# Branch A's projection in seven half-block products, its block sums added up in DRAM

## The chip, the cores and the metric

The kernel runs on one NeuronCore of a Trainium2 chip. The metric is the device time of one execution in microseconds (us). A core has a matrix engine (TensorE, PE in the profile; its weight loads are listed as PEld), a vector engine (VectorE, DVE), a scalar engine (ScalarE, ACT), a general engine (GpSimd, POOL) and an engine that issues transfers (SyncE, SP). Transfers issued by SP and by POOL are carried by 16 DMA engines. Each engine runs its own queue of instructions in order and waits on semaphores for the others.

## The reference

One layer of a streaming encoder is computed for 1024 prompt tokens and 32 sample tokens (1056 in all), model width 1024. The part around the change:

```
ya = attention(...)                      # branch A, 1024 wide (16 heads of 64)
yb = recurrence(...)                     # branch B, 1024 wide (8 heads of 128)
mix = sigmoid(ga) * (ya @ w_br_a) + sigmoid(gb) * (yb @ w_br_b)
x = x + rms_norm(mix @ w_out, g_post_mix)
```

After it come the feed-forward part (`w_up`, a short convolution, `w_down`) and a gated input. Everything is float32. `w_br_a` is 1024 x 1024.

## The kernel before

**Precision.** Every float32 operand is split into a high part (`hi`, rounded to the type that PE takes) and the rest (`lo`). A product takes three passes: hi x hi, hi x lo, lo x hi. `split` and the weight preparation do one copy on ACT and one subtraction on DVE for each operand.

**Layout.** Features lie on the 128 partitions, tokens along the free dimension. A 1024 wide operand is 8 row blocks (k), and the output is made in 8 column blocks (c) of 128 features. For the part after the branches the tokens are cut into four groups of 264 (`G4`, `H = 264`).

**Order.** The stages run one after the other, and PE is fed without a break between them:

1. Input norm, query/key/value products, attention head pair by head pair (i = 0 to 7), with gate products beside it. At the end of each i the result `ya` (128 x 1056) goes to DRAM (`ya_d`, L563).
2. Branch B: `w_in` for the recurrence in a scheme with fewer block products (`unit_pieces`), 8 heads, in small steps ("pieces"). Each head writes `yb_d` (L1384). Beside these pieces, POOL builds block sums of `w_down` in DRAM (`w_sums`, L1435 to 1443): 24 transfers from the weight itself and 8 from sums already built, the later ones adding to what lies there (`accum_op`). `behind(E, V, G)` queues an issue behind the last PE, DVE and POOL instruction written before it.
3. The last gate products (`tail`, three gate blocks before L1478 and three in `stream(tail[3:], small)`, L1485).
4. Branch A's projection (L1507 to 1522), the stage that is changed. `load_split` brings `ya_d` in 32 pieces of 128 x 264 and splits them into `Ra` and `Rb`. For each column block c and token group g a `block` of 8 row blocks times 3 passes = 24 matmuls goes to one of six PSUM banks. The weights are loaded 128 columns at a time (`next_w`, two blocks ahead). DVE then multiplies the bank with the gate (`ta_d`, loaded by SP) and POOL stores the result to `mx_d`. Beside it, `yb_d` is loaded and split into `Ya` and `Yb`.
5. Branch B's projection (L1544 to 1556): the same with `Ya`, `Yb`; the gated product is added to what `mx_d` holds and split into `Ra`, `Rb` again, the operands of `w_out`.
6. `w_out`, norms, the up projection (`up_unit`, 22 units) and the down projection (`d_unit`), both in seven products of half blocks, then the last gate and the output.

**The seven-product form.** A product of 2 x 2 blocks is made with seven block products in place of eight, at the price of sums of blocks on both sides ahead of it and of sums of results behind it. `OPS` puts products 0, 1, 2 in a first phase and 3 to 6 in a second. In the down projection the weight sums come from `w_d` and the operand sums from `s_d`; `d_unit` (L2263) runs one phase for one column block, with products 0 and 2, or 3 and 5, accumulating in the same PSUM double bank.

**Pages.** After attention the SBUF is cut into pages of 8 x 264 floats a partition, eight on the right (`rp`, r0 to r7, where branch B's tiles lay) and eight on the left (`lq`, l0 to l7, where the split input lay). A tile on a page waits until the tiles that had its memory before are released. A tile with `bufs=n` rotates through n buffers in the same way.

Of the kernel before, what the change touches and what calls it, by code (L numbers as in the profile page):

```python
# [59 lines left out]
def layer_kernel(  # L60
# [54 lines left out]
    ya_d = [dp.tile([P, T], F32, name=f"ya_d{i}") for i in range(8)]  # L115
    yb_d = [dp.tile([P, T], F32, name=f"yb_d{i}") for i in range(8)]
    ta_d = [dp.tile([P, T], F32, name=f"ta_d{i}") for i in range(8)]
    tb_d = [dp.tile([P, T], F32, name=f"tb_d{i}") for i in range(8)]
    mx_d = [dp.tile([P, T], F32, name=f"mx_d{i}") for i in range(8)]
# [41 lines left out]
    plan += [rows_cols(w_br_a, 0, c * P, P, KT) for c in range(8)]  # L161
# [151 lines left out]
    with right("ap") as ap:  # L313
# [226 lines left out]
        def values(i, js):  # L540
# [21 lines left out]
            if js[-1] == 8:  # L562
                dma(ya_d[i][:], ya[:])  # L563
# [513 lines left out]
    with right("bp") as bp:  # L1077
# [297 lines left out]
        def group_out(h, g):  # L1375
# [8 lines left out]
            dma(yb_d[h][:, o:o + n], sg[:, :n])  # L1384
# [44 lines left out]
        def more():  # L1429
            limit[0] = n_mix  # L1430
            load_next()
# [5 lines left out]
        for n, (o, a, h, other) in enumerate(w_sums):  # L1437
            for c in range(4):
# [4 lines left out]
                at(8 + 5 * (4 * n + c), w_sum)  # L1443
        for m, (run, ev) in enumerate(pieces):
# [12 lines left out]

    def page(pool, n, shape, name):

        return pool.tile(shape, F32R, tag=f"pg{n}", name=nm(name))  # L1460

    def columns8(pool, n, name):

        t = page(pool, n, [P, 8, H], name)
        return [t[:, k, :] for k in range(8)]
# [3 lines left out]
    def mt(tag, bufs):  # L1469
        return mp.tile([P, H], F32, tag=tag, name=nm(tag), bufs=bufs)  # L1470

    def load_split(src, hi, lo, g, k):
        o, n = G4[g]
        t = mt("ld", 8)
        dma(t[:], src[k][:, o:o + n])
        split(hi[g][k], lo[g][k], t[:])

    with right("mp") as mp:  # L1478
        Ra = [columns8(rp, 2 * g, "Ra") for g in range(4)]
        Rb = [columns8(rp, 2 * g + 1, "Rb") for g in range(4)]  # L1480
        small = {}
        for n in range(32):
            small.setdefault(n * 2 // 11, []).append(
                lambda n=n: load_split(ya_d, Ra, Rb, n // 8, n % 8))
        stream(tail[3:], small)  # L1485
        lctx.close()
        pctx.close()
# [5 lines left out]
        pq = qctx.enter_context(  # L1493
            tc.tile_pool(name="pq", bufs=1, space=PSUM, reuse_waits="tile"))

        def mm_bank():
            return bank(pq, "mm", 6)
# [4 lines left out]
        def block(w, wsl, xh, xl, ks, n):  # L1502
            b = mm_bank()
            product(b[:, :n], w, wsl, xh, xl, ks)
            return b
# [38 lines left out]
        for c in range(8):  # L1544
            if c % 2:
                p_cols(c // 2)
# [1118 lines left out]
```

## Time and profile before

| | us |
|---|---|
| runs shown | 1964.16, 1960.82, 1966.80 |
| median | 1964.16 |
| profiled execution | 1962.71 |
| its span, first to last instruction | 1960.9 |
| mean granted clock of PE | 0.998 |

The profile is of one execution. Its span is 1.8 us shorter than the execution's time; the rest is start and end. A row of the timeline gives the start in us from the span's start, the duration, the engine, the line of the kernel, the operation, the tiles (out<-in) and the shapes, and in brackets how long the engine sat idle before and what ended that. A row of the groups gives the count, then the time in which at least one of them was busy and the mean duration of one in ns, then the idle time of the engine just before them. Matmuls overlap on PE, so the duration of one is longer than the distance from one start to the next. Attention stores its eight results between 119 and 347 us of the span, branch B its results between 444 and 839; branch A's projection runs from 850 to 943, branch B's from there to about 1037.

### The profile page before, as it was taken

The numbers are of one execution on the slowest core, as the hardware profiler recorded it, in microseconds if no ns is written. First come the engines' busy times: TensorE is split into PE (matmuls) and PEld (weight loads), VectorE is DVE, ScalarE is ACT, GpSimd is POOL, SyncE is SP. The second block draws the span as 40 slices with busy tenths as digits, with TensorE's granted clock in tenths as the row PEclk, the third lists the DMA queues.
The fourth block names the chain that finished last, engine by engine and source line by source line (L and its number), as shares of the span: only waits on it lengthen the run. The fifth ranks groups of instructions, "written<-read, shape, count | busy, mean of one in ns | idle before, by whom it ended". The sixth has DMA issues, their size and how long they took to land. (4 is left out here: it accounts for less than half of the span.)

```text
span 1960.9 us, 38386 instructions
## 1 busy us (share of the span) xinstructions
PE 1938.8 (99%) x14715; PEld 1921.4 (98%) x14715; DVE 1432.0 (73%) x3174; ACT 997.9 (51%) x2182; POOL 299.7 (15%) x423
## 2 busy tenths in 40 slices
PE   8999999999999999999999999999999999999998
PEld 7999999999999999999999999999999999999998
DVE  6777777888888888654455778778778786668872
ACT  7667767666656666542224664333333346534432
POOL 2111111011102000002001023343333410000000
PEclk9999999999999999999999999999999999999999
DMA  8533433434549531477558582333323347655443
GB/s 269 148 102 99 128 109 118 156 106 117 115 106 168 110 87 36 136 229 236 167 166 296 174 296 62 111 101 109 110 94 118 96 159 248 206 183 160 120 132 89
DMA packets 296125, 283.12 MB, mean 144 GB/s; under 512 B 14885, under 2 KB 266184, under 8 KB 295941
## 3 DMA queue, kind: packets, MB, share of 16 engines
q1 hardware_dynamic: 270117, 224.80, 37.0%
q0 software_dynamic: 25696, 55.80, 11.7%
q8 instruction: 116, 1.90, 0.4%
q14 instruction: 68, 0.56, 0.1%
q10 hardware_dynamic: 128, 0.06, 0.0%
HBM read 195.46 MB, written 100.28 MB: 151 GB/s over the span
## 5 line engine op out<-in xcount | busy, mean ns | idle before, releaser
L2099 PE MATMUL st<-op,wt 128*128 128x264 f32 x1232 | 349.7, 284 | 3.8 <-ACT Sp L2110 1.7
L2101 PE MATMUL st<-op,wt 128*128 128x264 f32 x1232 | 350.4, 285 | 0.0
L2100 PE MATMUL st<-op,wt 128*128 128x264 f32 x1232 | 348.4, 283 | 0.0
L2099 PEld LDWEIGHTS st<-op,wt 128*128 128x128 f32 x1232 | 231.9, 188 | 5.6 <-ACT Sp L2110 2.3
L2100 PEld LDWEIGHTS st<-op,wt 128*128 128x128 f32 x1232 | 232.1, 188 | 0.0
L2101 PEld LDWEIGHTS st<-op,wt 128*128 128x128 f32 x1232 | 231.6, 188 | 0.0
L2218 PE MATMUL st<-dop,wt 128*128 128x264 f32 x616 | 174.4, 283 | 1.7 <-ACT S L2233 1.7
L2220 PE MATMUL st<-dop,wt 128*128 128x264 f32 x616 | 174.3, 283 | 0.0
L2219 PE MATMUL st<-dop,wt 128*128 128x264 f32 x616 | 173.9, 282 | 0.0
L1763 ACT CAST wt<-wu 128x512 fp32r<-128x512 f32 x126 | 75.9, 619 | 178.1 <-POOL ab L2085 75.5
L201 PE MATMUL mm<-La,wh 128*128 128x384 f32 (+1 forms) x480 | 158.2, 330 | 0.0
L202 PE MATMUL mm<-Lb,wh 128*128 128x384 f32 (+1 forms) x480 | 155.3, 324 | 0.6 <-DVE Lb L771 0.6
L203 PE MATMUL mm<-La,wl 128*128 128x384 f32 (+1 forms) x480 | 154.9, 323 | 0.1
L201 PE MATMUL mm<-Ra,wh 128*128 128x264 f32 x512 | 145.4, 284 | 0.0
L202 PE MATMUL mm<-Rb,wh 128*128 128x264 f32 x512 | 145.0, 283 | 0.0
L203 PE MATMUL mm<-Ra,wl 128*128 128x264 f32 x512 | 145.0, 283 | 0.0
L1764 DVE TENSOR_TENSOR wt<-wu,wt 128x512 fp32r<-128x512 f32 x126 | 86.4, 694 | 46.7 <-ACT wt L1763 46.7
L2218 PEld LDWEIGHTS st<-dop,wt 128*128 128x128 f32 x616 | 115.6, 188 | 2.2 <-ACT S L2233 1.9
L2219 PEld LDWEIGHTS st<-dop,wt 128*128 128x128 f32 x616 | 115.7, 188 | 0.0
L2220 PEld LDWEIGHTS st<-dop,wt 128*128 128x128 f32 x616 | 115.4, 187 | 0.0
L202 PEld LDWEIGHTS mm<-Rb,wh 128*128 128x128 f32 x512 | 96.5, 188 | 0.0
L201 PEld LDWEIGHTS mm<-Ra,wh 128*128 128x128 f32 x512 | 96.4, 188 | 0.0
(577 smaller groups left out, 6005.8 us busy)
## 6 DMA issues: line engine op xcount, KB each, us to landing
wu<-in_w_up_dram SPq DMA_DIRECT2D x42, 512.0 KB
wu<-in_w_in_dram SPq DMA_DIRECT2D x36, 512.0 KB
w_d<-in_w_down_dram POOLq DMA_DIRECT2D x24, 704.0 KB, 10.5
a_d<-Up SPq DMA_DIRECT2D x22, 528.0 KB
wr<-in_w_in_dram SPq DMA_DIRECT2D x21, 512.0 KB
s_d<-sm SPq DMA_DIRECT2D x40, 264.0 KB
dop<-s_d SPq DMA_DIRECT2D x16, 528.0 KB
wr<-in_w_out_dram SPq DMA_DIRECT2D x16, 512.0 KB
```

Of the source, the lines that this page charges most:

```text
L201: E.matmul(ps, wh, a, start=first and n == 0, stop=False)
L202: E.matmul(ps, wh, b, start=False, stop=False)
L203: E.matmul(ps, wl, a, start=False, stop=last and n == len(ks) - 1)
L1763: S.copy(t[:, 0], src)
L1764: V.tensor_tensor(t[:, 1], src, t[:, 0].bitcast(F32), op=ALU.subtract)
L2099: E.matmul(o, wh, xh, start=first and k == 0, stop=False, skip_group_check=True)
L2100: E.matmul(o, wh, xl, start=False, stop=False, skip_group_check=True)
L2101: E.matmul(o, wl, xh, start=False, stop=k == 3, skip_group_check=True)
L2218: E.matmul(o, wh, xh_, start=first and k == 0, stop=False, skip_group_check=True)
L2219: E.matmul(o, wh, xl_, start=False, stop=False, skip_group_check=True)
L2220: E.matmul(o, wl, xh_, start=False, stop=k == ng - 1, skip_group_check=True)
```

## The change

The product `ya @ w_br_a` is cut into 2 x 2 blocks: the 8 row blocks k into two halves (a), the 8 column blocks into two halves (h), and the tokens of each pair of groups t into two halves of 264 (h). It is then made in seven products of half blocks, each of 4 row blocks, for 4 column blocks c and 2 token pairs p. In `a_unit` one weight of 4 row blocks x 128 columns meets one operand of 4 row blocks x 264 tokens in 12 matmuls.

- **Operand sums.** At the end of each head pair in attention, ACT makes negated copies of two 264-token pieces in the two gate buffers (`gtile`), and SP stores them in `sa_d` (24 stores). During branch B, POOL adds the other blocks with five transfers from DRAM to DRAM (`y_sums`), four of them adding.
- **Weight sums.** Eight such transfers build the four sums of `w_br_a` blocks in `wa_d` (`a_sums`), four adding. The 13 transfers stand at every twelfth piece from piece 10 on.
- **Operands.** `a_load` brings 14 operand halves (7 products, 2 token pairs) straight onto pages, eight of them in the last three gate blocks, the other six in the first steps of the stage; `a_split` splits them in place.
- **Weights.** `a_raw` loads two half weights at a time, `a_prepare` splits them up to five ahead. `more` now stops at the gate weights (`n_gates`), and branch B's projection weights are asked for in steps 30 and 32 of 34.
- **Order.** The first two column blocks of phase 0 run for token pair 0 and then for pair 1 (12 half steps), then column blocks 2 and 3, then phase 1. Three PSUM double banks (`st`) replace the six single ones.
- **Results.** DVE combines the products, multiplies by the gate and either stores to `mx_d` (half of the output, through POOL) or keeps the gated result in SBUF (`M_`).
- **Branch B's projection.** Its operands are loaded straight onto pages in steps 18 to 21 and 31 to 32 and split in place, the last ones within branch B's first blocks; the first two column blocks run group by group. It reads `mx_d` for half of the blocks and `M_` for the other half.

The diff, cut to its core:

```diff
@@ attention, values() @@
             if js[-1] == 8:
-                dma(ya_d[i][:], ya[:])
+                dma(ya_d[:, i], ya[:])
+                for p in range(2):
+                    nt, o = gtile(), H * (2 * p + 1 - i // 4)
+                    S.mul(nt[:, :H], ya[:, o:o + H], -1.0)
+                    for q in ((4, 3) if i < 4 else (5,)):
+                        dma(sa_d[q][:, i % 4, p], nt[:, :H])
@@ branch B, beside its pieces @@
+        a_sums = [(3, av[:, 0, 0], 0), (4, av[:, 0, 1], 0), (1, av[:, 0, 0], 0), (6, av[:, 1, 0], 0),
+                  (3, av[:, 0, 1], 1), (4, av[:, 1, 1], 1), (1, wa_d[4][:], 1), (6, wa_d[1][:], 1)]
+        y_sums = [(4, ya_v[:, 0, 0], 1), (3, ya_v[:, 1, 1], 1), (1, sa_d[4][:], 0),
+                  (1, ya_v[:, 1, 1], 1), (5, sa_d[1][:], 1)]
+        for n, (dst, (o, src, acc)) in enumerate([(sa_d, y) for y in y_sums] + [(wa_d, a) for a in a_sums]):
+            def a_sum(dst=dst[o], src=src, op={"accum_op": ALU.add} if acc else {}):
+                with behind(E, V, G):
+                    gdma(dst[:], src, max_dma_last_dim=4224, **op)
+            at(10 + 12 * n, a_sum)
@@ the last gate blocks @@
+    at_a = {0: ("r6", "r5"), 1: ("r1", "r7"), 2: ("r3", "r4"), 3: ("r0", "r2"), 4: ("l0", "l1"),
+            5: ("l2", "l3"), 6: ("l4", "l5")}
+    def a_raw():
+        k = len(raw_a)
+        t = wp.tile([P, KT, P], F32, tag="wr", name=nm("wa"), bufs=2)
+        raw_a.append(t)
+        for a in range(2):
+            c, i = A_ORDER[2 * k + a]
+            src = wa_d[i] if i in wa_d else av[:, i // 2 % 2 + i // 5, i // 5]
+            dma(t[:, 4 * a:4 * a + 4], src[:, :, c * P:(c + 1) * P])
...
+    def a_load(i, p):
+        t = opa[i, p] = page_at(at_a[i][p], [P, 2, 4, H], "oa")
+        src = sa_d[i][:, :, p] if i in sa_d else ya_v[:, min(i, 1), i // 6][:, :, p]
+        dma(t[:, 1].bitcast(F32), src)
+    small = {0: [lambda i=i, p=p: a_load(i, p) for p in range(2) for i in range(3)]}
+    small[0] += [lambda p=p: a_load(3, p) for p in range(2)]
+    for m in range(4):
+        p, i = divmod(m, 3)
+        small.setdefault(m + 2, []).append(lambda i=i, p=p: both(a_split, i, p))
+    for m in range(3):
+        small.setdefault(m + 1, []).insert(0, lambda m=m: both(a_prepare, m))
+    stream(tail[3:], small)
@@ the stage @@
+        def a_unit(ph, c, tps=(0, 1), ws=None, beside=None):
+            X, Y = (pa.tile([P, 2, 512], F32, tag="st", name=nm("st"), bufs=3) for _ in range(2))
+            banks = {0: (X, True), 1: (Y, True), 2: (X, False), 3: (X, True), 4: (Y, True),
+                     5: (X, False), 6: (Y, False)}
...
+            for n, i in enumerate(OPS[ph]):
...
+                    a_prepare(n_a[0] + 5)
...
+                for p in tps:
+                    o, x = t[:, p, 0:H], opa[i, p]
+                    for k in range(4):
+                        E.matmul(o, w[:, 0, k], x[:, 0, k], start=first and k == 0, stop=False,
+                                 skip_group_check=True)
...
+                if i == 0:
+                    d["s"], d["ta"] = tmp("as"), a_gate(c, 0, sl)
+                    S.copy(d["s"][:, sl], x)
+                elif i == 1:
+                    V.tensor_tensor(r, x, d["s"][:, sl], op=ALU.subtract)
+                elif i == 2:
+                    ta = d["ta"]
+                    V.scalar_tensor_tensor(ta[:, sl], ta[:, sl], 1.0, x, op0=ALU.add, op1=ALU.mult)
+                    gdma(mx_d[:, 0, c, sl], ta[:, sl])
...
+        for n, (i, p) in enumerate((i, p) for i in (4, 5, 6) for p in range(2)):
+            during(2 * n, a_load, i, p)
+            during(9 + n + n // 2, both, a_split, i, p)
+        for n, (i, p) in enumerate(((1, 1), (2, 1), (3, 0), (3, 1))):
+            during(n + n // 2, both, a_split, i, p)
+        for n in range(4):
+            during(18 + n, y_load, n // 2, n % 2)
+            during(23 + n, both, y_split, n // 2, n % 2)
+        for n in range(4):
+            during(31 + n // 2, y_load, 2 + n // 2, n % 2)
+        during(30, prefetch)
+        during(32, both, load_next)
...
+        ws = [a_unit(0, c, (0,), beside=beside) for c in range(2)]
+        for c in range(2):
+            a_unit(0, c, (1,), ws[c], beside)
+        for c in range(2, 4):
+            a_unit(0, c, beside=beside)
+        for c in range(4):
+            a_unit(1, c, beside=beside)
```

216 lines of the change are left out of this document (147 added, 69 removed).

## Prediction

> **What bounds the kernel now.** The page's busy times come first, then the granted clock.
>
> ```profile
> PE 1938.8 (99%) x14715; PEld 1921.4 (98%) x14715; DVE 1432.0 (73%) x3174; ACT 997.9 (51%) x2182; POOL 299.7 (15%) x423
> PEclk9999999999999999999999999999999999999999
> ```
>
> TensorE (PE) is busy for 99% of the span at a full clock. Busy time alone does not prove that it is dense, because matmuls overlap in the pipeline, so the second view is the timeline of PE at both ends of the branch A projection (start, duration, engine, line, operation), and the third the groups inside it.
>
> ```profile
> 850.00 0.28 PE L201 MATMUL mm<-Ra,wh 128*128 128x264 f32 x1
> ...
> 942.81 0.28 PE L201 MATMUL mm<-Ya,wh 128*128 128x264 f32 x1
> ```
> ```profile
> L201 PE MATMUL mm<-Ra,wh 128*128 128x264 f32 x256 | 72.6, 284 | 0.0
> L202 PE MATMUL mm<-Rb,wh 128*128 128x264 f32 x256 | 72.5, 283 | 0.0
> L203 PE MATMUL mm<-Ra,wl 128*128 128x264 f32 x256 | 72.5, 283 | 0.0
> ```
>
> The first row is the first matmul of branch A, the second the first one of branch B's projection. Between them lie 3 x 256 = 768 matmuls, so the stage lasts 92.81 us and one matmul costs 92.81 / 768 = 0.1208 us of the span. The 283 ns of the groups is the latency of one, not its cost; whoever takes it would promise 27 us. The last column (idle before) is 0.0: there is no wait in this stage. Every matmul taken out shortens the span, and every wait put in lengthens it.
>
> The fourth view gives stretches (from:to, length, then busy time with count for PE, PEld, DVE, ACT, POOL, then clock, DMA share, GB/s): attention, branch B, the last three gate blocks, and the projection in pieces.
>
> ```profile
> 119.00:385.00 266.00, 264.85 (x1845) 262.46 (x1844) 202.41 (x607) 191.81 (x500) 41.02 (x116) 1.00 0.43 125
> 385.00:838.00 453.00, 452.03 (x3025) 449.50 (x3024) 373.99 (x1042) 284.53 (x749) 48.05 (x73) 1.00 0.47 108
> 838.00:850.00 12.00, 12.00 (x77) 11.96 (x77) 5.21 (x12) 6.28 (x16) 0.00 (x0) 1.00 0.66 196
> 850.00:867.00 17.00, 17.00 (x142) 17.00 (x142) 12.86 (x32) 10.51 (x26) 1.65 (x4) 1.00 0.92 277
> 867.00:885.00 18.00, 18.00 (x151) 18.00 (x150) 7.98 (x18) 6.59 (x14) 3.22 (x6) 1.00 0.81 244
> 885.00:905.00 20.00, 20.00 (x168) 20.00 (x167) 12.18 (x26) 8.50 (x19) 3.76 (x7) 1.00 0.86 262
> ```
>
> Behind PE the next resource in this stage is the DMA engines: 0.92 busy in its first 17 us. That is where the change can give its gain back.
>
> **The change, part by part.** *Removed.* Seven products of 4 column blocks, 2 token pairs, 4 row blocks and 3 passes are 7 x 4 x 2 x 4 x 3 = 672 matmuls of the same shape. 96 go: 96 x 0.1208 = **11.6 us**. The loops fix this count, so I see no way for the change not to do what it says.
>
> [...]
>
> *Added at the opening.* The same seven-product scheme runs twice already. Its first waits, in the down projection and in the up projection (the brackets hold PE's idle time and what ended it):
>
> ```profile
> 1628.15 0.28 PE L2220 MATMUL st<-dop,wt 128*128 128x264 f32 x1
> 1630.11 0.39 PE L2218 MATMUL st<-dop,wt 128*128 128x264 f32 x1 [1.68 <-ACT S L2233]
> ```
> ```profile
> 1163.99 0.39 PE L2099 MATMUL st<-op,wt 128*128 128x264 f32 x1 [0.69 <-ACT ple L1739]
> 1166.44 0.39 PE L2099 MATMUL st<-op,wt 128*128 128x264 f32 x1 [0.73 <-ACT ple L1739]
> 1168.17 0.39 PE L2099 MATMUL st<-op,wt 128*128 128x264 f32 x1 [1.23 <-ACT Sp L2110]
> ```
> ```profile
> L2218 PE MATMUL st<-dop,wt 128*128 128x264 f32 x592 | 167.6, 283 | 1.7 <-ACT S L2233 1.7
> ```
>
> The down projection loses 1630.11 - 1628.15 - 0.12 = 1.8 us at its start and, in the rest of 3 x 592 matmuls, nothing (the 1.7 is that one wait). The up projection waits 2.7 us in three places, on ScalarE's (ACT's) copies out of PSUM. Why the scheme waits where eight plain products do not: product 2 accumulates onto product 0's bank and must wait for its copy, and three double banks replace six single ones. For the new opening I take 2.5 us, bounds 0 (the stage now opens without a wait) and 18 (below).
>
> *VectorE and ScalarE beside it.* The prices of one weight half, one operand half and one evacuation:
>
> ```profile
> L1870 ACT CAST wt<-wd 128x512 fp32r<-128x512 f32 (+1 forms) x84 | 49.0, 586 | 91.0 <-PE st L2220 80.0 <-DMA wd<-w_d 4.8 <-issue 2.6
> L1871 DVE TENSOR_TENSOR wt<-wd,wt 128x512 fp32r<-128x512 f32 (+1 forms) x84 | 53.0, 641 | 6.3 <-ACT wt L1870 6.3
> L2072 ACT CAST dop<-dop 128x1056 fp32r<-128x1056 f32 (+1 forms) x42 | 42.0, 1000 | 2.8 <-DMA dop<-a_d 2.6 <-DMA dop<-s_d 0.2
> L2073 DVE TENSOR_TENSOR dop<-dop 128x1056 fp32r<-128x1056 f32 (+1 forms) x42 | 48.7, 1162 | 14.4 <-ACT dop L2072 14.3
> L1519 DVE SCALAR_TENSOR_TENSOR ta<-ta,mm 128x264 f32<-128x264 f32 x32 | 13.5, 426 | 28.1 <-PE mm L203 16.2 <-DMA ta<-ta_d 11.8
> ```
>
> The first 12 steps are half steps of 12 matmuls, 12 x 12 x 0.1208 = 17.4 us. In them VectorE (DVE) has 8 weight halves, 6 operand halves and 8 evacuations: 8 x 0.641 + 6 x 1.162 + 8 x 0.426 = 15.5 us, or 89%, where it has 12.9 of 17 now. It fits, barely; after step 12 the steps are twice as long. At nothing, therefore, but inside the 2.5.
>
> *DMA of the stage.* Sizes and counts of today's issues:
>
> ```profile
> w_d<-in_w_down_dram POOLq DMA_DIRECT2D x24, 704.0 KB, 10.5
> w_d<-w_d POOLq DMA_DIRECT2D x8, 704.0 KB, 6.7
> wd<-w_d SPq DMA_DIRECT2D x32, 256.0 KB
> ld<-ya_d SPq DMA_DIRECT2D x32, 132.0 KB
> dop<-s_d SPq DMA_DIRECT2D x16, 528.0 KB
> ```
>
> Operands grow from 32 x 132 KB (4.3 MB) to 14 x 528 KB (7.6 MB), weights from 8 x 512 KB (4.2 MB) to 28 x 256 KB (7.3 MB); the gates stay at 4.3 MB, and branch A's stored part halves from 4.3 to 2.2 MB, written once and read once. With branch B's operands (4.3 MB) and next weights (1.3 MB) some 27 MB go through in 81 us (672 x 0.1208) and the 12 us ahead, near 290 GB/s, against the 244 to 277 of the rows. So a part has to come earlier, or the queue runs late. A load can start when the memory of its page is free. Branch B's tiles set that: its block-sum operands (`TH`, `TL`) are last read at 816.6, its output tiles (`sg`) only after 838.7 (first and last start of each group).
>
> ```profile
> L1111 PE MATMUL Y<-TL,wt x216: 333/334/346, 358.7 to 816.6; 128*128 128x384 f32 x108
> L1382 DVE SCALAR_TENSOR_TENSOR sg<-tr,ghh,sg x24: 499/602/771, 443.3 to 838.7; 128x384 f32<-128x384 f32 x16, 128x288 f32<-128x288 f32 x8
> ```
>
> The eight pages (67.6 KB a partition) cover the eight tiles `TH` and `TL` (49.2 KB) and 18.4 KB of the tiles beside them, so about five of them are free some 20 us before the other three. On SP's queue today the loads come behind branch B's last store:
>
> ```profile
> 839.29 0.38 SPq L1384 DMA_DIRECT2D yb_d<-sg  x1
> 839.77 2.31 SPq L1475 DMA_DIRECT2D ld<-ya_d  x5
> ...
> 845.98 0.42 SPq L1517 DMA_DIRECT2D ta<-ta_d  x1
> ```
>
> The last row shows a gate load that overtook `ld` loads waiting for buffers, so the order on SP follows readiness, and I take it that five operand halves are loaded early. The three left at 839.8 (1.6 MB, 6 us at 277 GB/s) land ahead of their products from 850.
>
> *Block sums.* 13 transfers of about 1.06 MB on POOL's queue in branch B; by bytes from the rows above each takes 6.7 to 10.5 x 1.06 / 0.72 = 10 to 15 us, in all 130 to 200 of 453 us. The branch already carries 32 smaller ones and PE is busy 452.03 of 453; DMA share would go from 0.47 to at most 0.9. POOL issues 13 more:
>
> ```profile
> L1442 POOL DMA_DIRECT2D w_d<-in_w_down_dram x24 | 32.2, 1518 | 1.1 <-issue 0.8
> ```
>
> 13 x 1.5 = 20 us more of POOL beside its 48 of 453; memsets and copies queue behind, and PE's banks cover them. I charge 0.5 us, bounds 0 and 8 (third rival). If the cover is gone, a late weight half stops PE.
>
> *Attention.* 16 negated copies on ACT and 24 small stores on SP. A scaled copy of this shape:
>
> ```profile
> L1651 ACT ACTIVATE z<-x,gvec 128x264 f32<-128x264 f32 x28 | 12.3, 508 | 2.1 <-DVE x L1641 2.1
> ```
>
> 16 x 0.508 = 8 us, ACT being busy 191.81 of 266, so they fit. Each also borrows one of the two gate buffers until its stores land; the gate copy and the exponentials queue behind it on ACT. 0.3 us, bounds 0 and 4.
>
> *Hand-over to branch B.* The first two of its weights are prepared in the last four steps (11.6 us), two copies and two subtractions beside PE: 0.4 us, bounds 0 and 3.
>
> **Sum.** -11.6 + 2.5 + 0.5 + 0.3 + 0.4 = -7.9. The profiled execution took 1962.7 (span 1960.9 and 1.8 around), giving 1954.8; the median of the runs, 1964.2, would give 1956.3. I say **1955.5**.
>
> **The rivals.** *First, the gate loads become the wait.*
>
> ```profile
> DVE ta L1519 <- DMA ta<-ta_d: 11.8, 8, 3.6
> ```
>
> Today DVE waits 8 times, 11.8 us in all, for a gate tile. Six banks of one product each (24 x 0.1208 = 2.9 us) hide it. The new evacuation of product 2 needs the same loads, its bank is wanted again one half step (1.45 us) later, and behind it on DVE stand the weight subtractions and every other evacuation. Against it: gate loads overtake others already. If half of these waits reach PE: 5.9 more, 1961.
>
> *Second, the opening is bound by DMA and the kernel gets slower.* Place: steps 0 to 12. If no page is free early, the queue holds from 839.8 the 8 + 6 operand halves (7.6 MB), 10 weight halves (2.6), gates, stores and gate writes (1.7): 11.9 MB at the mean of 277 and 244, 260 GB/s, take 46 us, until 885.6; step 12 is due at 867.4. 18 us late replace the 2.5: 1955.5 + 15.7 = 1971. It decides at 10.4 us late (the 2.5 charged and the 7.9 left), that is, by whether some operand halves are issued before 839: five of them are 2.7 MB, 10 us. For it speaks the 0.92 of the first 17 us; against it the reordering on SP. [...]
>
> *Third, the sums hold up branch B's weights.* Where transfers bunch, one of 10 to 15 us stands before weights asked for about half a unit (12 us) ahead: two such places at 4 us give 8, 1963. PE's 452.03 beside 32 such transfers speaks against it. [...]
>
> **How the numbers follow.** About 0.3%, 5.9 us, is what a measurement of this kernel can tell from no change; faster means below 1958.3. Forecast 0.60 (its own range 1950.5, all waits hidden, to 1958), first rival 0.18, third 0.08, second 0.14. Faster 0.60, same 0.26, slower 0.14. The range goes from 1950 to 1967: below it little is possible with 11.6 removed, above it lies most of the second rival.
>
> **What would show it.** Right: 672 matmuls at 0.121 us between branch A's first and branch B's first, a stage of 82 to 87 us, operand loads on SP before 839, a first wait of 1 to 4 us ended by ACT or DVE. Wrong: gaps in steps 0 to 12 ended by a DMA (second rival) or by DVE behind a gate load (first), or PE's busy time falling in attention or branch B.

## The result and the profile after

The changed kernel takes **1977.4 us** (median of four runs, 1976.8 to 1980.5) where the kernel before takes 1963.8 on the same chip (four runs, 1960.8 to 1966.8): a ratio of 1.0072, 95% interval 1.0054 to 1.0091. The forecast was 1955.5, the range 1950 to 1967. The profiled execution took 1977.9 us, its span 1976.2, which is 15.3 us more than the span before.

The busy times and the granted clock of the page, as they were shown of before:

```profile
PE 1935.5 (98%) x14619; PEld 1916.4 (97%) x14619; DVE 1452.8 (74%) x3160; ACT 1011.4 (51%) x2182; POOL 300.8 (15%) x414
PEclk9999999999999999989999999999999999999999
```

96 matmuls are gone (14715 to 14619), and PE's busy time barely falls, by 3.3 us. It falls little because PE waits and then runs at a lower clock, and a matmul at half clock counts as busy for longer: a product of the new stage (L1599, 128x264) lasts 422 ns at a clock of 0.50 (878.02 to 881.44 us) and 284 at 1.00 (881.44 to 884.85). The timeline of PE shows the waits, in brackets:

```profile
381.48 0.66 PE L1118 MATMUL Z<-La,wt 128*128 128x384 f32 x1 [5.12 <-DVE tf L1146]
397.68 0.44 PE L1118 MATMUL Y<-TH,wt 128*128 128x384 f32 x1 [2.15 <-DVE vt L1139]
693.76 0.58 PE L1367 MATMUL so<-z,z 128*128 128x128 f32 x1 [4.85 <-DVE S L1347]
876.57 0.59 PE L1597 MATMUL st<-oa,wt 128*128 128x264 f32 x1 [7.76 <-ACT gt L297]
894.20 0.36 PE L1597 MATMUL st<-oa,wt 128*128 128x264 f32 x1 [0.65 <-DVE R L1608]
961.18 0.28 PE L205 MATMUL mm<-Ya,wh 128*128 128x264 f32 x1
```

Three of the four long waits lie in branch B, not in the stage that was rewritten, and the fourth is at that stage's first matmul. Beside three of them PE's granted clock is halved. The view of these three stretches (from:to, length, busy time with count for PE, PEld, DVE, ACT, POOL, then clock, DMA share, GB/s):

```profile
379.68:386.51 6.83, 5.03 (x16) 5.07 (x17) 5.10 (x9) 2.96 (x6) 0.00 (x0) 0.50 0.41 103
693.71:697.12 3.41, 3.36 (x13) 3.36 (x14) 3.41 (x10) 2.77 (x9) 0.00 (x0) 0.50 0.34 92
871.20:881.44 10.24, 4.87 (x22) 4.87 (x23) 3.06 (x4) 5.11 (x8) 0.00 (x0) 0.50 0.95 282
```

PE worked 5.0, 3.4 and 4.9 us at a clock of 0.50, so about 2.5 + 1.7 + 2.4 = 6.6 us went to the clock (an estimate: half of each).

The 15.3 us by stage, from the first matmul of each: branch B starts at 357.3 us instead of 354.9 (+2.4); it lasts from there to the last gate matmul 511.1 us instead of 494.9 (+16.2); the opening gap is 8.1 us instead of 0.2 (+7.9); branch A's stage lasts 84.6 instead of 92.8 (-8.2); everything behind it is 3.4 us shorter, most of it in the up projection (454.7 us instead of 457.9). The sum is +15.0 before rounding, and the last 0.3 us lie behind the last matmul.

**Where the four waits come from.** First, the start of branch B. POOL's timeline and the waits of ACT:

```profile
334.32 1.49 POOL L1460 DMA_DIRECT2D sa_d<-ya_d  x1
335.14 1.80 POOL L1451 DMA_DIRECT2D w_d<-in_w_down_dram  x1
...
355.96 1.45 POOL L1460 DMA_DIRECT2D sa_d<-ya_d  x1 [17.83 <-DMA ya_d<-ya]
356.97 2.59 POOL L1451 DMA_DIRECT2D w_d<-in_w_down_dram  x2
```
```profile
ACT wt L1039 <- DMA wu<-in_w_in_dram: 10.5, 1, 10.5
```

The second sum of `y_sums` reads the last head pair's result. POOL stood 17.83 us for it with two `w_d` transfers behind it, and then sent all three just as SP asked for branch B's next weights. One weight then kept ACT waiting 10.5 us. The view of transfers for 357 to 385 us, of after and then of before, shows what was in the way (queue, packets, MB, share of the 16 engines):

```profile
q1 hardware_dynamic: 4853, 4.62, 54.5%
q0 software_dynamic: 1424, 2.52, 42.7%
```
```profile
q1 hardware_dynamic: 4565, 3.04, 36.3%
```

q0 holds POOL's transfers here and q1 SP's: before, POOL moved nothing in this stretch.

Second, at 688 us. POOL's timeline, and the chain of waits:

```profile
661.42 1.18 POOL L1460 DMA_DIRECT2D wa_d<-in_w_br_a_dram  x1
662.06 1.38 POOL L1451 DMA_DIRECT2D w_d<-w_d  x1
670.57 0.88 POOL L1460 DMA_DIRECT2D wa_d<-wa_d  x1 [7.13 <-DMA wa_d<-in_w_br_a_dram]
671.12 2.00 POOL L1451 DMA_DIRECT2D w_d<-w_d  x2
682.25 0.59 POOL L1324 DMA_DIRECT2D S<-in_state_hgrn_dram  x1 [9.12 <-PE so L1369]
```
```profile
682.28 10.97 DMA out_dram<-S
693.36 0.36 DVE S L1347
693.76 0.80 PE so L1367 x2
```

The recurrence of branch B keeps a state `S` of 64 KB, which is stored and loaded again. Here its store took 10.97 us, and the load issued beside it 8.0 where it takes 2.2 at the median. Third, the opening. SP's timeline and ACT's:

```profile
857.92 0.38 SPq L1393 DMA_DIRECT2D yb_d<-sg  x1
859.91 0.37 SPq L1529 DMA_DIRECT2D oa<-ya_d  x1
...
863.98 3.35 SPq L1529 DMA_DIRECT2D oa<-sa_d  x2
867.43 2.83 SPq L298 DMA_DIRECT2D tb_d<-gt  x2
```
```profile
876.02 0.49 ACT L297 ACTIVATE gt<-Z 128x384 f32<-128x384 f32 x1 [7.79 <-DMA tb_d<-gt]
```

No operand load went out early; all eight stand behind branch B's last store, and the gate stores stand behind them. ACT's last gate copy needs one of two gate buffers and waited for such a store.

### The profile page after: what moved, and what is told of

Read it like the earlier page. It is cut to its first block, busy times and chain, and to the rows that moved or that the text cites. A ratio compares the mean times of both kernels' runs of the same rounds, so it can differ in the third digit from the quotient of the medians.

```text
span 1976.2 us, 38048 instructions
## 1 busy us (share of the span) xinstructions
PE 1935.5 (98%) x14619; PEld 1916.4 (97%) x14619; DVE 1452.8 (74%) x3160; ACT 1011.4 (51%) x2182; POOL 300.8 (15%) x414
## 4 chain that ended last, share of the span: by engine, by line
PE 77%; DVE 9%; DMA 6%; ACT 4%; issue 3%; POOL 0%; SPq 0%; ACTq 0%; DVEq 0%; POOLq 0%
PE st L2278 7%; PE st L2276 7%; PE st L2277 7%; PE mm L205 5%; PE mm L207 5%; PE mm L206 5%; PE st L2395 4%; PE st L2397 4%; PE st L2396 4%; DMA wu<-in_w_in_dram 2%; PE G L1121 2%; PE G L1120 2%; PE G L1118 2%; PE Y L1118 2%; PE Y L1121 2%
## 5 line engine op out<-in xcount | busy, mean ns | idle before, releaser
L1944 ACT CAST wt<-wu 128x512 fp32r<-128x512 f32 x126 | 75.9, 618 | 178.1 <-POOL ab L2262 75.5
L1945 DVE TENSOR_TENSOR wt<-wu,wt 128x512 fp32r<-128x512 f32 x126 | 86.4, 694 | 46.7 <-ACT wt L1944 46.7
L2050 ACT CAST wt<-wd 128x512 fp32r<-128x512 f32 (+1 forms) x84 | 49.1, 586 | 91.2 <-PE st L2397 69.5
L1039 ACT CAST wt<-wu 128x512 fp32r<-128x512 f32 x108 | 64.8, 617 | 58.1 <-DVE wu L1047 25.3
L1040 DVE TENSOR_TENSOR wt<-wu,wt 128x512 fp32r<-128x512 f32 x108 | 72.5, 685 | 27.2 <-ACT wt L1039 26.9
L206 PEld LDWEIGHTS mm<-Lb,wh 128*128 128x128 f32 x480 | 90.5, 189 | 1.7 <-DVE Lb L780 1.4
L205 PEld LDWEIGHTS mm<-La,wh 128*128 128x128 f32 x480 | 90.3, 188 | 0.7 <-DVE pl L229 0.6
```

What stands on the lines that cost most here:

```text
L205: E.matmul(ps, wh, a, start=first and n == 0, stop=False)
L206: E.matmul(ps, wh, b, start=False, stop=False)
L1945: V.tensor_tensor(t[:, 1], src, t[:, 0].bitcast(F32), op=ALU.subtract)
```

## The experiments

All kernels are the changed one with the edit shown, timed beside the kernel before on the same chip. The table holds the median, the ratio to before with its interval, and from one profiled run of each, in us: branch B from its first matmul (B) and from its first matmul on the block sums `TH` (B2; the 500 and 491 in the expectations from e11_paced_free on count so), the opening gap, gap and stage A together, and the time at half clock between 300 and 1000 us.

| kernel | median | ratio | B | B2 | gap | gap + A | half clock |
|---|---|---|---|---|---|---|---|
| before | 1961.8 to 1963.8 | | 494.9 | 491.3 | 0.2 | 93.0 | 0 |
| changed | 1977.4 | 1.0072 (1.0054 to 1.0091) | 511.1 | 507.5 | 8.1 | 92.7 | 20.5 |
| e1_gate_stores | 1976.1 | 1.0075 (1.0058 to 1.0092) | 511.9 | 508.2 | 1.1 | 88.1 | 17.1 |
| e2_late_sum | 1979.5 | 1.0091 (1.0076 to 1.0106) | 512.2 | 505.6 | 8.1 | 94.3 | 20.5 |
| e3_state_sp | 1984.1 | 1.0115 (1.0100 to 1.0131) | 516.9 | 513.2 | 8.4 | 91.9 | 27.3 |
| e4_no_sums | 1963.9 | 1.0015 (1.0006 to 1.0025) | 494.3 | 490.6 | 8.2 | 91.5 | 13.7 |
| e6_paced | 1971.6 | 1.0051 (1.0031 to 1.0070) | 503.7 | 500.0 | 8.4 | 92.9 | 10.2 |
| e8_loads_pool | 1983.2 | 1.0107 (1.0092 to 1.0122) | 513.9 | 510.2 | 11.2 | 96.0 | 27.3 |
| e9_paced_loads | 1973.5 | 1.0058 (1.0043 to 1.0073) | 502.5 | 498.9 | 11.0 | 94.7 | 13.7 |
| e10_free_pages_first | 1977.1 | 1.0081 (1.0062 to 1.0100) | 512.9 | 509.2 | 5.2 | 91.0 | 20.5 |
| e11_paced_free | 1969.0 | 1.0031 (1.0021 to 1.0042) | 503.3 | 499.6 | 5.3 | 90.6 | 6.8 |
| e12_paced_free_state | 1967.0 | 1.0024 (1.0014 to 1.0035) | 507.1 | 503.5 | 2.3 | 85.5 | 3.4 |
| e13_weights_ahead | 1975.2 | 1.0078 (1.0062 to 1.0093) | 510.9 | 507.2 | 1.9 | 85.3 | 10.2 |
| e14_split_paced | 1964.5 | 1.0013 (1.0004 to 1.0022) | 502.2 | 498.5 | 4.0 | 87.0 | 10.2 |
| e15_split_paced_state | 1965.3 | 1.0023 (1.0012 to 1.0033) | 504.1 | 500.4 | 1.2 | 84.6 | 6.8 |
| e16_all_paced | **1956.8** | **0.9971** (0.9960 to 0.9982) | 496.4 | 492.8 | 1.8 | 85.2 | 0 |
| e17_all_paced_state | 1957.9 | 0.9973 (0.9963 to 0.9983) | 500.6 | 496.9 | 1.2 | 84.0 | 3.4 |

### One suspected cause at a time

**e1_gate_stores.**

```diff
-        u, v = (unit(gate_out(dst)) for dst, _ in GATES[14:])
+        u, v = (unit(gate_out(dst, gdma)) for dst, _ in GATES[14:])
```

> The six stores of the last gate blocks go out on POOL's DMA queue instead of SP's; nothing else is edited. Theory (the opening waits because two of these stores stand on SP's queue behind eight operand loads, so the third gate copy on ScalarE waits 7.79 us for its buffer): the gap between the last gate matmul and the first matmul of branch A falls from 7.9 us to 1 to 3 us, the 10 us of half clock around it go, and the time falls by 7 to 10 us, to 1967.5 to 1970.5. Rival (the opening is bound by the DMA engines, the operand and weight loads themselves come late): a gap of 6 us or more stays, ended by an oa or wa load, and the time stays within 2 us of 1977.4.

The gap falls from 8.1 to 1.1 us, as the theory has it, but a second wait appears, and gap and stage together fall by 4.6 us only. PE's timeline, then ACT's, then a stretch of the opening:

```profile
877.86 0.46 PE L1597 MATMUL st<-oa,wt 128*128 128x264 f32 x1 [2.53 <-ACT wt L1520]
```
```profile
877.19 0.62 ACT L1520 CAST wt<-wa 128x512 fp32r<-128x512 f32 x1 [0.47 <-DMA wa<-wa_d]
```
```profile
861.00:876.00 15.00, 13.54 (x91) 13.01 (x90) 7.79 (x9) 8.66 (x14) 1.53 (x3) 1.00 1.06 353
```

The engines are full for 15 us (share 1.06, 353 GB/s, more than any row of before's stage), and a weight half that SP issued at 867.9 us lands only at 877.2. So theory and rival both hold a part of this wait. The time is no better than the changed kernel's beyond the intervals. Of the 4.6 us, 2.0 were lost again in the up projection (456.7 us instead of 454.7), where PE ran at half clock for 3.4 us in this run and not in the changed kernel's.

**e2_late_sum.** `at(10 + 12 * n, a_sum)` becomes `at(34 if n == 1 else 10 + 12 * n, a_sum)`.

> The one block sum that reads the last head's output (sa_d of operand 3 += heads 4 to 7) is issued 12 steps later, so it no longer stands at POOL's queue in front of two w_d copies. Theory (POOL stood 17.8 us behind the last head's store, and then three large transfers ran against branch B's first weights): the gaps at 376 to 381 us (5.3) and 395 to 398 us (2.3) go, with the 6.8 us of half clock after the first, and the time falls by 8 to 11 us, to 1966.5 to 1969.5. Rival (the added bytes in branch B slow its first weights wherever they stand, or the late end of attention does it): the gaps stay or move, and the time falls by less than 3 us.

The 5.12 us and the 2.15 us go. PE's timeline shows others in their place:

```profile
364.08 0.44 PE L1118 MATMUL Y<-TH,wt 128*128 128x384 f32 x1 [2.77 <-ACT gt L297]
450.13 0.38 PE L1367 MATMUL so<-z,z 128*128 128x128 f32 x1 [1.51 <-DVE S L1347]
694.24 0.58 PE L1367 MATMUL so<-z,z 128*128 128x128 f32 x1 [5.59 <-DVE S L1347]
```

The sum now goes out at 422 us, with a `w_d` transfer just ahead of it and another new sum just behind it, and the wait at 450 us is for a state load (3.7 us in the waits of DVE). The rival's "move" is what happened: the one bad place was not the whole cause.

**e3_state_sp.** `gdma(d["S"][:], ...)` becomes `dma(d["S"][:], ...)`.

> The eight loads of the state (S, 64 KB each) go out on SP's queue instead of POOL's, where they stand behind the large transfers. Theory (transfers of one queue are served in turn, and the load issued at 682.25 us lands after 8 us because three transfers stand before it): the load takes 2 to 3 us, the 5.0 us gap at 688.6 and the 3.4 us of half clock after it go, and the time falls by 5 to 7 us, to 1970.5 to 1972.5. Rival (the DMA engines are full there, whichever queue asks): the load still takes 5 us or more and the time falls by less than 2 us.

The rival holds. The chain of waits at 688 us:

```profile
685.49 2.56 SPq L1352
688.09 5.23 DMA S<-in_state_hgrn_dram
693.42 0.36 DVE S L1347
```

The load still takes 5.23 us, and SP needed 6.9 us to issue the store ahead of it. Taking the load off POOL's queue does not take the wait away. The row of after could have told this: its 10.97 us store was on SP's queue already. Branch B even became longer, by 5.8 us.

**e4_no_sums.** The 13 transfers are not issued; `a_raw` and `a_load` read unsummed blocks of the same sizes, so the output is not the layer's and only the time counts.

> Leaves the 13 block sums in DRAM out; branch A reads unsummed weights and operands of the same sizes. Theory (all that branch B lost, 16.2 us, comes from where these transfers stand in POOL's queue): branch B is back to 495 us, the gaps at 376, 395 and 688 us go, the gap of 7.9 us at branch A's opening stays, and the time is 1960 to 1963. Rival (the negated copies and stores in attention delay branch B's start by themselves): a gap of 2 us or more stays at 376 us, and the time is 1965 to 1970.

Branch B is back at 494.3 us and the opening gap stays. **All of branch B's loss comes from the 13 transfers.** What the theory did not have is a loss at the end of attention, in ACT's timeline:

```profile
344.28 0.42 ACT L570 ACTIVATE gt<-ya 128x264 f32<-128x264 f32 x1 [2.67 <-DMA tb_d<-gt]
```

A negated copy waits 2.67 us for a gate buffer, whose gate store (SP issued two from 335.34 us on) had not landed; POOL had sent five old `w_d` transfers between 332 and 338 us. The copies behind it on ACT, the split of the last softmax among them, start at 344.61 us or later. So the rival's point, a delay by the copies, came true in attention and not at 376 us. This run starts branch B at 360.6 us (before 354.9), and its time of 1963.9 is 0.9 over the expected band.

### Pacing the transfers

POOL's queue has little of branch B's work in it, so `behind(E, V, G)` places a transfer in POOL's order but not in time. In the next kernels a transfer waits for a copy of one element that ACT makes at the same piece.

**e6_paced.**

```diff
+        def pace():
...
+            with behind(E, S, V, G):
+                S.copy(pace_a[0:1, i:i + 1], ident[0:1, 0:1])
+                G.tensor_copy(pace_g[0:1, i:i + 1], pace_a[0:1, i:i + 1])
...
+                    pace()
                     with behind(E, V, G):
                         gdma(w_d[o][:, c], src, **op)
...
+                pace()
                 with behind(E, V, G):
                     gdma(dst[:], src, max_dma_last_dim=4224, **op)
```

> Every transfer of the block sums (the 13 new ones and the 32 for the down projection) first waits on POOL for a one-element copy that ScalarE makes at the same step of branch B, so POOL can no longer send several in a row; same transfers, same order, same bytes. Theory (it is the bunches: several megabytes in a row on the 16 engines delay stores and loads of 64 to 512 KB that land in 2 to 5 us otherwise): the start of branch B is back at 358 to 359 us, the gaps at 376, 395 and 688 us go, branch B takes 493 to 498 us, the opening of branch A stays as it was, and the time falls by 13 to 18 us against the changed kernel, to 1959 to 1964. Rival (the added bytes themselves): the gaps move instead of going, as in the kernel with the late sum, branch B stays above 503 us, and the time falls by less than 6 us.

The start of branch B is back (354.5 us), the waits at 376, 395 and 688 us are gone, and no half clock is left before the opening. But branch B still takes 503.7 us, in the rival's range: many waits of 0.5 to 2 us remain, the longest on a state load right behind one 1 MB transfer:

```profile
442.71 0.38 PE L1369 MATMUL so<-z,z 128*128 128x128 f32 x1 [1.96 <-DVE S L1349]
```

About half of branch B's loss is taken back (8.8 us stay of 16.2), so the expected band (1959 to 1964) was missed, and the size of one transfer or the bytes stayed open.

### The opening

**e8_loads_pool.** The eight `a_load` of the last gate blocks are called with `put=gdma`. **e9_paced_loads** is the same on top of e6_paced.

> The first eight operand loads of branch A are issued on POOL's queue, which has nothing else there, instead of SP's, where they stand behind branch B's last stores; the gate stores stay on SP. Theory (the pages are free early and only SP's order kept the loads until 859.9 us): at least five loads are issued before 850 us, the gap at the opening is under 2 us, no DMA wait follows, the opening and stage A together fall from 92.7 us to 83 to 86 us, and the time falls by 7 to 11 us, to 1966 to 1970. Rival (the pages are not free earlier, so the opening is bound by the DMA engines whatever the queue): the loads go out at 858 us or later, the opening and stage together stay at 87 us or more as in the kernel with the gate stores on POOL (88.1 us), and the time falls by 2 to 5 us.

> Both edits together: the sums paced by ScalarE, and the first eight operand loads on POOL's queue. Theory: the two losses are separate and add, so the time falls by 20 to 28 us against the changed kernel, to 1949 to 1957, faster than the kernel before. Rival: the paced sums end later and stand on POOL ahead of the operand loads, or POOL's pace holds the loads up; then the opening keeps its 7.9 us and the time is no better than with the pacing alone.

Both got worse at the opening (gaps of 11.2 and 11.0 us). The rival of e8_loads_pool holds in its place (the loads go out at 863 us), but the time rose by 6 us where it had 2 to 5 less. That of e9_paced_loads holds in its outcome and not in its cause: POOL's idle time before the first load ends as in e8_loads_pool, whose timeline of POOL says why:

```profile
863.24 0.78 POOL L1529 DMA_DIRECT2D oa<-ya_d  x1 [16.70 <-DMA yb_d<-sg]
```

The first load's page lies where branch B's last `sg` tile lay, and waits for its store. Five of the eight pages lie over `TH` and `TL`, by the count of the prediction, and three over tiles that branch B uses until its end; the first load in the queue has one of these three. The other seven were written behind it and went out right after it, from 864.00 us on.

**e10_free_pages_first.** The late pages go to the loads that are needed last. The names of the pages stay; which memory a page gets follows the order of the calls, as the loads of the two kernels show: the first one called waited for `sg` in e8_loads_pool, and here two of the first three do (SP's waits have 1.4 us for `yb_d<-sg`).

```diff
-    small = {0: [lambda i=i, p=p: a_load(i, p) for p in range(2) for i in range(3)]}
-    small[0] += [lambda p=p: a_load(3, p) for p in range(2)]
+    small = {0: [lambda i=i, p=p: a_load(i, p) for i, p in ((3, 0), (3, 1), (2, 1))]}
+    small[0] += [lambda i=i, p=p: a_load(i, p, gdma) for i, p in ((0, 0), (1, 0), (2, 0), (0, 1), (1, 1))]
```

> Of the first eight operand loads the three that are needed last take the three pages that branch B's last tiles still hold, and stay on SP's queue; the five needed first take the pages that lie wholly over the block-sum operands TH and TL, and go out on POOL's queue, which is idle there. Theory (five pages are free 20 us early, as the prediction took it, but the first page in the queue was one of the three late ones and held all the others): the five loads go out between 817 and 850 us, the opening's 7.9 us fall to under 2, opening and stage A together take 83 to 87 us instead of 92.7, and the time falls by 6 to 10 us against the changed kernel, to 1966 to 1970. Rival (the gate stores' place on SP alone made the wait, and early loads only move the DMA's rush elsewhere): opening and stage stay at 88 us or more, with waits that a DMA ends.

The five loads go out at 845 us, so they could go early. The gap is still 5.2 us. ACT's timeline:

```profile
874.05 0.62 ACT L1520 CAST wt<-wa 128x512 fp32r<-128x512 f32 x1 [4.41 <-DMA wa<-wa_d]
874.58 0.48 ACT L297 ACTIVATE gt<-Z 128x384 f32<-128x384 f32 x1
```

ACT stood in front of the gate copy for a weight half, which SP issued at 867 us behind the three late loads. The rival holds by its numbers (91.0 us), by another load than it named.

**e11_paced_free** is e10_free_pages_first with e6_paced's pacing, **e12_paced_free_state** has the state loads on SP's queue too.

> The free pages first, and the block sums paced by ScalarE as in the kernel with paced sums. Theory: the gains add (7 to 8 us from the pacing, 6 to 10 us from the opening): 1958 to 1963, level with the kernel before, because the paced branch B still takes 500 us where it took 491. Rival: the paced sums end later and hold POOL when the five loads should go; then the opening gap stays above 5 us.

> As the kernel before it in this list, with the eight state loads on SP's queue too. Theory (what is left of branch B's loss is small loads behind one 1 MB transfer on the same queue; the state load at 434 us took 8 us with a single transfer ahead of it): the two waits for the state (2.1 us at 440, 1.3 us at 736) go, and the time falls by 2 to 4 us more. Rival (the engines are shared, the queue is not what counts, as the state loads on SP showed in the bunched kernel): no change beyond 1 us.

e11_paced_free missed its band by 6 us, because the opening kept 5.3 us. That is the number of its rival, but not its cause: the five loads went out at 833 us, and ACT stood 4.47 us for a weight half as in e10_free_pages_first. In e12_paced_free_state the time falls by 2.0 us, the low end of its theory, but by luck: the waits for the state stay (1.97 us at 443), branch B is 3.8 us longer, and what fell is the opening's gap, by 3 us, which the theory did not name.

**e13_weights_ahead.** The three late loads move from `small[0]` to the end of `small[3]`, behind the weight halves; their pages are taken ahead of the others as before.

> As the kernel with the free pages first (five operand loads on POOL at 845 us), but the three operand loads that are needed last are issued three half blocks later, so SP's queue has the third and fourth weight halves and the gate stores ahead of them. Theory (the 5 us that stayed at the opening were a weight load issued only at 867 us behind those three loads, for which ScalarE stood 4.4 us in front of the last gate copy): the opening's gap falls from 5.2 to under 2 us, opening and stage A together take 83 to 88 us (92.7 in the changed kernel, 91.0 with the free pages first). Rival (the weight halves wait for their own raw buffers, not for the queue): the gap stays at 4 us or more.

The gap is 1.9 us, gap and stage together 85.3: the theory holds. The median of four runs hides it (1970.5 to 1979.8; the profiled run was the first of these), since branch B was untouched. That branch B varies from run to run would explain it and is not shown, as one execution of each kernel was profiled; over the seven kernels with unpaced sums it takes 510.9 to 516.9 us.

### Down to small transfers

**e14_split_paced** adds to e13_weights_ahead the pacing of the new transfers alone, each cut into four; **e15_split_paced_state** has the state loads on SP's queue.

```diff
+            for k in range(4):
...
+                    pace()
+                    with behind(E, V, G):
+                        gdma(dst[:, k], src[:, k], max_dma_last_dim=4224, **op)
+                at(10 + 3 * (4 * n + k), a_sum)
```

> As the kernel before it in this list, with each of the 13 new transfers cut into four of 264 KB, each of them paced by ScalarE (the 32 transfers of the down projection stand between them in POOL's order and are not paced themselves). Theory (what is left of branch B's loss in the paced kernels, 500 us against 491, is small loads and stores that wait for one 1 MB transfer at a time): branch B takes 492 to 497 us and the time is 1953 to 1960. Rival (it is the added bytes or the added POOL and ScalarE instructions): branch B stays at 499 us or more.

> As the kernel before it, with the state loads on SP's queue. Theory: with no large transfer in the way, the queue of the state loads makes no difference: within 2 us of the kernel before it. Rival (POOL's order holds the state loads up): 2 to 4 us less.

e14_split_paced missed its bands for the time (1964.5) and, by B2, for branch B (498.5, just under the rival's 499). But branch B's loss is one single wait and the half clock around it, in PE's timeline, with SP's and ACT's behind it:

```profile
587.75 0.58 PE L1329 MATMUL so<-vk,kk 128*128 128x128 f32 x1 [3.93 <-ACT vk L1372]
```
```profile
570.80 19.30 SPq L1216 DMA_DIRECT2D tb_d<-gt  x4
```
```profile
586.15 0.52 ACT L1215 ACTIVATE gt<-x 128x384 f32<-128x384 f32 x1 [7.01 <-DMA tb_d<-gt]
```

A bunch was left: seven transfers between 560 and 572 us, three of them of the unpaced 704 KB kind, and a gate store of 192 KB took 15 us beside them. e15_split_paced_state is within 2 us of it, as the theory has it, though not because nothing moved: branch B is 1.9 us longer and the opening's gap 2.8 us shorter. In e14_split_paced that gap is 4.0 us again, and ACT stood 2.45 us of it for a weight half.

**e16_all_paced** paces the 32 old transfers too and spreads all of them a tenth wider (`at(8 + 11 * (4 * n + c) // 2, w_sum)`, `at(10 + 13 * (4 * n + k) // 4, a_sum)`); **e17_all_paced_state** has the state loads on SP's queue.

> As the kernel with split and paced sums, with the 32 transfers of the down projection paced too and all of them spread a tenth wider over branch B. In the run before it, one bunch was left: seven transfers of 2.9 MB in all between 560 and 572 us, and a gate store issued at 570.8 us landed after 15.3 us, for which TensorE stood 4.1 us and then ran at half clock for 7 us. Theory (bunches, and nothing else, make branch B's loss): this gap goes, branch B takes 490 to 494 us, and the time falls by 5 to 9 us against that kernel, to 1955 to 1960, below the kernel before by 2 to 6. Rival (more pacing only shifts the queue, because POOL's order holds up state loads and memsets): branch B stays at 498 us or more.

> As the kernel before it, with the state loads on SP's queue, where POOL's waits for its pace cannot hold them up. Theory: within 2 us of the kernel before it. Rival: 2 to 4 us less, since POOL now waits more.

Both theories hold by their numbers. The stretches of branch B from B2's start, and of opening and stage A, of e16_all_paced:

```profile
359.40:852.20 492.80, 491.91 (x3265) 488.96 (x3264) 400.41 (x1087) 314.48 (x871) 132.84 (x220) 1.00 0.66 148
852.20:939.00 86.80, 83.87 (x688) 83.15 (x688) 60.70 (x83) 33.73 (x48) 5.46 (x10) 1.00 0.83 256
```

PE is busy 491.91 of 492.80 us with all the transfers beside it, 84 by now (32 old ones, and 13 new ones in four parts each). So the added bytes as such cost at most the 1.5 us by which branch B is longer than before. Which of the two edits, the pace or the wider spread, took the last bunch away was not separated.

The kernel is **0.29% faster than before** (0.18 to 0.40%): the change pays once its transfers are small and held to their places, and the opening's loads are ordered by when their pages are free. Branch B of the kernel before, at 494.9 us with its transfers unpaced, is no longer than this one, so the gain does not lie there. It lies in opening and stage A, which take 85.2 us instead of 93.0. A paced kernel before was not run.

In all four pairs that differ in the queue of the state loads alone, branch B is longer with the loads on SP's queue: by 5.8 us in e3_state_sp and by 3.8, 1.9 and 4.2 us in e12, e15 and e17. In e17_all_paced_state the last state load is issued at 830.0 us where POOL issued it at 826.9 in e16, and PE waits 2.24 us behind it. So by one profiled run of each the queue did matter, against the edit.

## Why the prediction was wrong

| term of the sum | predicted, us | measured, us |
|---|---|---|
| 96 matmuls | -11.6 | -11.6 |
| opening of the new stage | 2.5 | 11.3 |
| block sums in branch B | 0.5 | 16.2 |
| attention | 0.3 | 2.4 |
| hand-over to branch B's projection | 0.4 | 0 |
| behind it | none | -3.4 |

- **Removed matmuls: right.** 672 are left, and 672 x 0.1208 = 81.2 us; the stage's 84.6 are these, the wait of 0.65 at 894 us, 2.4 to the clock, and 0.4 in small waits.
- **"I charge 0.5 us" for the block sums: the step that failed most.** The price of one transfer was right (10 to 15 us forecast; 11.0 to 12.6 at the medians of the sums, though one took 30.8). The cover was not. PE's "452.03 beside 32 such transfers" was read as room for 13 more, but a DMA share of 0.47 is a mean; nothing in it says that POOL sends them one at a time. The third rival named the mechanism, weights and loads behind a bunch, with two places at 4 us; there were three, with 5.1, 2.2 and 4.9 us, and 4.2 us of half clock on top, which makes up the 16.2. Its price of 8 us was half of what came, and its chance of 0.08 put it last of the rivals.
- **"I take it that five operand halves are loaded early": wrong in the order, and the second step that failed.** Five pages were free early, as worked out: in e11_paced_free five loads went out at 833 us, 16 us ahead of branch B's last store. But that SP's order "follows readiness" rested on one gate load that overtook others. The first load in the queue had one of the three late pages, so none went out before 859.9 us. The second rival's point ("whether some operand halves are issued before 839") decided as it said, and its place was right: the engines were full for 15 us (share 1.07 from 861 to 876 us of the changed kernel). Its price of 18 us was too high for the opening alone; 7.9 of gap, 0.6 of wait and 2.4 of clock came.
- **First rival.** The gate loads did not become the wait; the gate stores did, through the two gate buffers. In e4_no_sums a wait in attention has the same cause: the prediction saw that the negated copies borrow these buffers, and priced it at 0.3. The 2.4 us of the table are of one execution. In the other kernels' profiled runs, with the same copies, branch B starts at 354.5 to 360.6 us, and at 354.9 in e3_state_sp, whose program is the same up to there. So the 2.4 us can be the difference of two executions.
- **The second and the third rival were taken as alternatives.** Both came true at once. The range reaches to one or the other, and so it ended at 1967.
- **The clock.** Half clock lasts 6.83, 3.41 and 10.24 us in the changed kernel, two, one and three times 3.41, and the prediction's sum has no term for it. The trace of the kernel before shows it too, right behind the three waits of the up projection that the prediction quotes (the second row):

```profile
1165.93:1169.34 3.41, 1.68 (x11) 1.46 (x12) 1.87 (x3) 2.06 (x4) 0.75 (x1) 1.00 1.05 370
1169.34:1172.75 3.41, 3.41 (x18) 3.41 (x17) 1.26 (x1) 3.39 (x4) 0.00 (x0) 0.50 1.13 323
```

  So the up projection's opening cost 2.7 us of waits and about 1.7 us by the clock (an estimate: half of the 3.41 us at 0.50), and a price of 2.5 us for such an opening was short even by the rows that it came from.
- **Queues.** In e3_state_sp the state load took 5.23 us from SP's queue, after 8.0 from POOL's in the changed kernel, where its median is 2.2. The other queue did not free it of its wait.
- **Behind stage A.** Of the 3.4 us, 3.2 lie in the up projection, of which the change moves the pages and no more. In before's profiled execution its waits are 1.3 us longer in all, and the half clock above costs another 1.7. Whether the pages or the one execution made this stays open. In the other kernels' profiled runs the part behind stage A is between 3.7 us shorter and 0.3 us longer than before.
- **A small slip.** The lower end of the forecast's own range, "1950.5, all waits hidden", does not come out of the sum: 1962.7 - 11.6 is 1951.1, and 1964.2 - 11.6 is 1952.6.
- **What stays open.** Of the attention's 2.4 us only the wait for the gate buffer was seen, and a kernel with a third buffer was not run.

## What to carry to other kernels

Before transfers are hidden beside a busy engine, look at when their queue will really send them: on an engine with little other work, places in the order are not places in time. In the changed kernel five transfers of 704 or 1024 KB went out between 661 and 673 us, and a 64 KB store issued at 682.28 took 10.97 us. Pace them by something that runs with the bottleneck, keep each one small, and look for operations that have only two buffers and wait for a small store to free one. For early loads, look which page the first one in the queue gets, not how many are free.

## What was not expected of the hardware

- Half clock came behind a short wait too. In e12_paced_free_state the wait was 1.97 us, and PE had been busy 1.45 of the 3.41 us ahead; the stretches ahead of and during the half clock:

```profile
440.16:443.57 3.41, 1.45 (x9) 1.12 (x8) 0.58 (x3) 1.25 (x6) 0.00 (x0) 1.00 0.10 40
443.57:446.98 3.41, 3.41 (x14) 3.41 (x15) 3.41 (x10) 2.37 (x7) 0.00 (x0) 0.50 0.07 22
```

- In e13_weights_ahead a wait of 2.31 us, from 393.8 to 396.2 us, was followed by a full clock. It lies across two stretches of 3.41 us, and PE was busy 2.45 and 2.06 us in them:

```profile
391.40:394.81 3.41, 2.45 (x17) 2.21 (x16) 3.41 (x11) 2.42 (x6) 0.00 (x0) 1.00 0.00 0
394.81:398.22 3.41, 2.06 (x12) 2.06 (x13) 3.41 (x8) 3.41 (x9) 0.00 (x0) 1.00 0.00 0
```

So the length of the wait alone does not decide: half clock followed the 1.97 us and not the 2.31. In the changed kernel the three stretches at half clock begin at 379.68, 693.71 and 871.20 us, 92 and 52 times 3.413 us apart. In the 3.41 us ahead of each, at a clock of 1.00, PE was busy 0.08, 0.00 and 1.02 us; ahead of the one shown of the kernel before it was busy 1.68 us, and ahead of the one in e12_paced_free_state 1.45. In the last 3.41 us of each of these five PE was busy 3.36 to 3.42 us, and the clock was 1.00 again behind it. What sets the clock was not shown. The wait of 1.97 us cost about 1.7 us more by the clock (an estimate: half of the 3.41 us at 0.50), the one of 2.31 us nothing more.
